# Forming the first two channel tiles together, reordering the turn to the down projection, and halving the last output tile

## The chip, the core and the metric

The kernel runs on one core of one Trainium2 chip. A core has TensorE (PE in the profile; PEld is its weight load, which overlaps), VectorE (DVE), ScalarE (ACT), GpSimd (POOL) and SyncE (SP), which here only issues transfers. Each engine takes its instructions in order and waits for others through semaphores. Operands lie in SBUF (128 partitions); matmul results lie in PSUM, in banks of 128 x 512 float32. The metric is the device time of one execution in microseconds; shorter is better.

## The reference

One transformer-like block on x (1024 tokens by 1024), in float32:

```python
h = rms_norm(x, norm1_g[l])
z = h @ w_in[l]
glu_in, q, k, v, gate_logits = jnp.split(z, SPLITS, axis=-1)
a_val, a_gate = jnp.split(glu_in, 2, axis=-1)
a = a_val * jax.nn.sigmoid(a_gate)
a = causal_depthwise_conv(a, conv_w[l], conv_b[l])          # 31 taps
a = jax.nn.silu(rms_norm(a, conv_norm_g[l]))
y_a = a @ w_conv_out[l]
...
y_b = o @ w_attn_out[l]          # o: dilated attention, 16 heads, 3 groups
g_a, g_b = jnp.split(jax.nn.sigmoid(gate_logits + gate_b[l]), 2, axis=-1)
x = x + (g_a * y_a + g_b * y_b) @ w_out[l]

h = rms_norm(x, norm2_g[l])
u = causal_depthwise_conv(h @ w_up[l], ffn_conv_w[l], ffn_conv_b[l])   # 3 taps
u_val, u_gate = jnp.split(u, 2, axis=-1)
x = x + (jax.nn.silu(u_gate) * u_val) @ w_down[l]
```

## The kernel before, in words

**Precision.** Each float32 operand of a product is split into a rounded high part and the rest (`split`, lines 77 to 80: ACT rounds, DVE subtracts). A product is three matmuls: high by high, high by low, low by high. So nearly every weight or activation costs one ACT and one DVE instruction before PE can use it. A "step" below is one such matmul, 128x128 by 128x512.

**Order.** A planner in the build lays out the order of each engine's instructions by a simulated timeline. In three stretches the order of ACT, DVE and PE is the written one (`tc.manual_schedule`): the start (line 432), attention (line 770) and the change to the feed-forward part (line 1038). `tc.issue_after(i)` ties what it encloses, on i's engine only, behind i in the order of issue; it adds no wait for i to finish.

**Start (lines 287 to 502).** The gated linear unit has eight channel tiles c of 128 channels, each with a gate part g and a value part v. For c = 0 and 1, and the first half of the tokens, PE multiplies raw x (scaled by the norm's gain) and the norm's factor is applied at the end. x arrives in eight blocks k (`xT`, 256 KB each). `w_first` holds the weights of tile 0 in four pieces, each for two k; piece 0 is loaded in two halves of columns, g and v. `raw_high`/`raw_low` (lines 363 and 366) split x's block k, `weights(k)` splits the weights of k and k+1 in four blocks of 256 columns (`whigh` line 381, `wlow` line 384; the profile shows their instructions at L382 and L386). `pair` (line 390) issues the steps of tile c, at L395. Tile 0 goes k by k as the blocks arrive, six steps each; then tile 1, whose weights come in two whole loads (`stage`, L84), goes at once, 48 steps, with the norm's spread over the rows (`spread`, L347) after 36 of them. Then follow both tiles on the second half of the tokens, and tiles 2 to 7 with the loop at line 510. Rounded weights live in the tags `whi` and `wlo`, four buffers each; tiles 0 and 1 take all four, and the next tile's rounding takes a buffer when its last reader is done. While tiles 2 and up run, DVE scales and splits the first half of x (`normed` L371, `low` L375).

**Convolution and cover.** `conv_branch` (line 538) runs on DVE beside the q, k, v products. At its end PE sums squares (`pss`, line 656). `cover(n)` (line 644) takes n steps of three matmuls from a stock of side work (the gates' products, `side_steps`); `COVER` (line 39) gives the counts: before the convolution's end, after the sum, after the spread. The rest of the stock is spent inside attention. There, pieces of gate weights wait in a queue for their split; `piece_high` (line 167) rounds one, at two places of each slot; the first is taken if more than three wait (line 789).

**Up projection and turn.** Each up tile f (22 of them) is formed by a Strassen-like scheme of products (`product`, L979 to L981). `up_rest` (line 1157) ends one: its PSUM bank X is drained at L1168, multiplied into again (third product), read at L1172, multiplied into once more (fourth product, `t4`) and drained at L1177; Y is a second bank. `up_end` (line 1143) applies the three taps (L1148, L1150) and stores the tile. The down projection (from line 1221) multiplies in six groups of two f-tiles (the last of one). Its first sweep adds into X[0..3], which lie in two double banks `dx_0` and `dx_1`; `dx_1` is the memory of the last up tile's X and Z. For groups 0 and 1, loaded early, the steps for n = 0, 1 come before those for n = 2, 3 (lines 1272 to 1275): 24 steps are free of the last up tile and 24 wait for L1177. `gsplit` and `wsplit` round the groups' operands; those of group 4 are tied behind L1177 (line 1269).

**End (lines 1349 to 1358).** The steps of the last two groups are kept back: for n = 0 to 3 nine steps on Y[n], then for n = 0 to 3 the residual is loaded, nine steps on X[n] follow (`mac`, L1247), DVE adds (L1251) and SP stores the 128x512 tile (`emit`, L1279).

Of the kernel before, what the change touches and what calls it, by code (L numbers as in the profile page):

```python
# [21 lines left out]
P = 128  # L22
# [16 lines left out]
COVER = (14, 8, 20)  # L39
# [14 lines left out]
def block_kernel(ctx: ExitStack, tc: tile.TileContext, x, xT, x0, g2, pack, mask,  # L54
# [225 lines left out]
    with tc.tile_pool(name="ph1", bufs=1) as p1:  # L280
# [11 lines left out]
        raw0 = [wp.tile([P, 1024], F32, tag="raw", bufs=4, name=f"raw_gv{n}") for n in range(2)]  # L292
        block0 = lambda k, i: raw0[k // 4][:, (k // 2 % 2) * 512 + i * 256 : (k // 2 % 2) * 512 + i * 256 + 256]

        def first_weights(k):
            if k == 0:
                for i in range(2):
                    sp.dma_start(block0(0, i), w_first[0, :, i * 256 : i * 256 + 256])
            else:
                sp.dma_start(raw0[k // 4][:, (k // 2 % 2) * 512 : (k // 2 % 2) * 512 + 512], w_first[k // 2])  # L300
# [16 lines left out]
        raw1 = []  # L317
# [56 lines left out]
        def low(half, k):  # L374
# [3 lines left out]
        wfirst = [[[wp.tile([P, 1024], F32R, tag=t, bufs=4, name=f"{t}_{n}{c}") for t in ("whi", "wlo")] for n in "gv"]  # L378
                  for c in range(2)]

        def whigh(c, which, raw, cols=slice(0, 1024)):
            act.activation(wfirst[c][which][0][:, cols], raw, AF.Copy)  # L382

        def wlow(c, which, raw, cols=slice(0, 1024)):
            hi, lo = wfirst[c][which]
            dve.tensor_tensor(out=lo[:, cols], in0=raw, in1=hi[:, cols].bitcast(F32), op=ALU.subtract)  # L386
# [3 lines left out]
        def pair(c, half, ks, passes, which):  # L390
            w = [t.rearrange("p (a b) -> p a b", a=KT) for t in wfirst[c][which]]
            o = glu0[c, half][which]
            for k in ks:
                for wa, ha in passes:
                    pe.matmul(o, w[wa][:, k, :], hT[ha][half][:, k, :],  # L395
# [36 lines left out]
        with tc.manual_schedule(engines={ENG.Activation, ENG.DVE, ENG.PE}):  # L432
# [5 lines left out]
            def weights(k):  # L438
                c = slice(k * P, k * P + 2 * P)
                for i in range(2):  # L440
                    whigh(0, i, block0(k, i), c)
                    wlow(0, i, block0(k, i), c)
# [24 lines left out]
            pair(1, 0, b, HH + HL + LH, 1)  # L467
# [213 lines left out]
    with tc.tile_pool(name="ph2", bufs=1, reuse_waits="tile") as p2:  # L681
# [88 lines left out]
        with tc.manual_schedule(engines={ENG.Activation, ENG.DVE, ENG.PE}):  # L770
            pend = []
            for at in range(len(slots) + BACK + 1):
# [16 lines left out]
                if len(pieces) > 3:  # L789
                    piece_high(2)  # L790
# [351 lines left out]
    if True:  # L1142
# [14 lines left out]
        def up_rest(f, xz, sw, gw, s4):  # L1157
# [10 lines left out]
            act.activation(uv[:, t1], X, AF.Copy)  # L1168
# [7 lines left out]
            product(X, gh[:, 4:8], gl[:, 4:8], *blk["t4"], False)  # L1176
# [241 lines left out]
```

## Time and profile before

| what | us |
|---|---|
| median of 3 runs | 1747.04 (1746.75 to 1747.27) |
| profiled execution, its own time | 1747.08 |
| its span in the profile | 1745.3 |
| PE busy / PEld busy | 1738.5 / 1449.6 |
| DVE busy / ACT busy / POOL busy | 1298.5 / 796.6 / 176.3 |

The times in the lines are microseconds from the span's start; a row of the order of time has start, duration, engine, line, operation, tiles, shapes and, in brackets, how long the engine was idle before it and what released it. A matmul's duration is longer than its share of PE, since matmuls are pipelined: the share is the distance from one start to the next. The clock that PE was granted is full throughout (9 in each of 40 slices).

### The profile page before, as it was taken

What the parts mean: (1) busy time and instruction counts of PE and PEld (TensorE: products, weight loads), DVE (VectorE), ACT (ScalarE), POOL (GpSimd) and SP (SyncE); (2) the same over time, 40 slices, a digit from 0 to 9 for tenths busy, and PEclk for the clock granted to TensorE, in tenths of its full rate; (3) what the DMA queues carried; (4) which work ended last, traced back from release to release, by engine and by line L of the source; (5) the groups of instructions that cost most, each with busy time, mean ns of one, the idle gap of its engine ahead of it and who ended that gap; (6) DMA issues with size and microseconds to landing.
All of it is one profiled execution on the core that took longest, in us unless ns stands there. A gap on an engine that the chain in (4) does not pass through costs nothing.

```text
span 1745.3 us, 22811 instructions
## 1 busy us (share of the span) xinstructions
PE 1738.5 (100%) x8214; PEld 1449.6 (83%) x8214; DVE 1298.5 (74%) x1997; ACT 796.6 (46%) x1277; POOL 176.3 (10%) x188
## 2 busy tenths in 40 slices
PE   9999999999999999999999999999999999999999
PEld 7888888888888888888888888888888888878887
DVE  5999999999766666667654564787777776879863
ACT  6411233223276666667563342555445444543431
POOL 0000231132012222222200000000000000000000
PEclk9999999999999999999999999999999999999999
DMA  7111145345686556657356576632221222498851
GB/s 300 67 49 49 49 145 169 103 142 174 175 275 180 148 161 164 181 163 229 111 186 211 167 260 254 219 119 75 95 85 72 85 84 85 138 335 324 294 175 49
DMA packets 149202, 277.00 MB, mean 159 GB/s; under 512 B 12000, under 2 KB 61536, under 8 KB 149088
## 3 DMA queue, kind: packets, MB, share of 16 engines
q1 hardware_dynamic: 146784, 269.25, 47.5%
q10 hardware_dynamic: 2304, 6.29, 0.9%
q8 instruction: 65, 1.06, 0.3%
q14 instruction: 49, 0.40, 0.1%
HBM read 202.09 MB, written 73.40 MB: 158 GB/s over the span
## 4 chain that ended last, share of the span: by engine, by line
PE 98%; DMA 1%; DVE 0%; issue 0%; ACT 0%; SPq 0%; ACTq 0%
PE dx L1247 7%; PE xz L979 6%; PE xz L980 6%; PE xz L981 6%; PE dy L1247 5%; PE qkv L128 5%; PE qkv L130 5%; PE qkv L129 5%; PE pp L721 4%; PE gate L111 3%; PE gate L113 3%; PE gate L112 3%; PE y L980 2%; PE y L979 2%; PE y L981 2%; PE o L736 2%
## 5 line engine op out<-in xcount | busy, mean ns | idle before, releaser
L80 DVE TENSOR_TENSOR pl<-pp,ph 128x512 fp32r<-128x512 f32 (+2 forms) x191 | 100.3, 552 | 91.0 <-ACT ph L79 90.8
L128 PE MATMUL qkv<-hi_qkv,hT 128*128 128x512 f32 x384 | 150.9, 395 | 0.0
L130 PE MATMUL qkv<-hi_qkv,hT 128*128 128x512 f32 x384 | 150.2, 391 | 0.0
L129 PE MATMUL qkv<-lo_qkv,hT 128*128 128x512 f32 x384 | 149.9, 391 | 0.0
L79 ACT ACTIVATE ph<-pp 128x512 fp32r<-128x512 f32 (+2 forms) x191 | 86.7, 488 | 117.4 <-PE pp L721 116.1
L706 DVE CUSTOM_DVE_ANT_0 p<-s,m 128x128 f32<-128x128 f32 (+3 forms) x120 | 90.5, 754 | 43.6 <-PE s L702 39.9
L715 POOL TENSOR_SCALAR p<-p,st 128x128 f32<-128x128 f32 (+3 forms) x120 | 91.3, 761 | 279.9 <-DVE st L714 232.2
L1150 DVE SCALAR_TENSOR_TENSOR u<-u,pk 128x1023 f32<-128x1023 f32 x88 | 112.2, 1277 | 1.0 <-ACT u L1148 0.7
L111 PE MATMUL gate<-hT,hi_gt 128*128 128x512 f32 x256 | 102.3, 400 | 0.0
L112 PE MATMUL gate<-hT,hi_gt 128*128 128x512 f32 x256 | 100.4, 392 | 0.0
L113 PE MATMUL gate<-hT,lo_gt 128*128 128x512 f32 x256 | 100.4, 393 | 0.0
L104 POOL TENSOR_TENSOR rs<-ss,mhalf 128x8 f32<-128x8 f32 x32 | 67.8, 2121 | 297.3 <-DVE ss L103 297.3
L711 ACT ACTIVATE p<-p,st 128x128 f32<-128x128 f32 (+3 forms) x120 | 93.0, 775 | 2.1 <-DVE st L706 1.2
L560 DVE SCALAR_TENSOR_TENSOR cacc<-csum,both,cacc 128x512 f32<-128x512 f32 x120 | 89.3, 745 | 0.8 <-ACT cacc L558 0.4
L560 DVE SCALAR_TENSOR_TENSOR cacc<-apad,pk,cacc 128x512 f32<-128x512 f32 x120 | 87.4, 745 | 0.0
L130 PEld LDWEIGHTS qkv<-hi_qkv,hT 128*128 128x128 f32 x384 | 72.1, 188 | 15.0
L129 PEld LDWEIGHTS qkv<-lo_qkv,hT 128*128 128x128 f32 x384 | 72.2, 188 | 14.4
L560 DVE SCALAR_TENSOR_TENSOR codd<-apad,pk,codd 128x513 f32<-128x513 f32 x112 | 83.6, 747 | 0.4 <-ACT codd L553 0.4
L80 DVE TENSOR_TENSOR lo_uv<-raw_uv,hi_uv 128x1024 fp32r<-128x1024 f32 x20 | 24.5, 1225 | 79.8 <-ACT hi_uv L79 79.8
L128 PEld LDWEIGHTS qkv<-hi_qkv,hT 128*128 128x128 f32 x384 | 72.1, 188 | 14.1
L721 PE MATMUL pp<-ident,p 128*128 128x128 f32 x540 | 78.7, 272 | 0.0
L721 PEld LDWEIGHTS pp<-ident,p 128*128 128x128 f32 x540 | 65.8, 140 | 14.5 <-DVE op L747 0.2
(362 smaller groups left out, 4849.0 us busy)
## 6 DMA issues: line engine op xcount, KB each, us to landing
wr<-w_down SPq DMA_DIRECT2D x45, 512.0 KB, 5.8
gr<-dff SPq DMA_DIRECT2D x62, 256.0 KB, 5.1
raw_qkv<-w_qkv SPq DMA_DIRECT2D x24, 512.0 KB, 5.2
dff<-u SPq DMA_DIRECT2D x22, 512.0 KB, 2.6
raw_uv<-w_up SPq DMA_DIRECT2D x21, 512.0 KB, 3.2
raw_ug<-w_up SPq DMA_DIRECT2D x20, 512.0 KB, 3.2
dv<-v SPq DMA_DIRECT2D x16, 512.0 KB, 3.2
raw_gt<-w_ch SPq DMA_DIRECT2D x16, 512.0 KB, 4.2
```

The costliest lines, as they stand in the source:

```text
L111: pe.matmul(o, hi[:, k, :], ah[:, k, :], start=(k == 0), stop=False)
L112: pe.matmul(o, hi[:, k, :], al[:, k, :], start=False, stop=False)
L113: pe.matmul(o, lo[:, k, :], ah[:, k, :], start=False, stop=(k == KT - 1))
L128: pe.matmul(ps, ah, hi[:, k % 2, :], start=(k == 0), stop=False)
L129: pe.matmul(ps, ah, lo[:, k % 2, :], start=False, stop=False)
L130: pe.matmul(ps, al, hi[:, k % 2, :], start=False, stop=(k == KT - 1))
L560: dve.scalar_tensor_tensor(out=out_, in0=src[:, i : i + size], scalar=w(i), in1=out_, op0=ALU.mult, op1=ALU.add)
L721: pe.transpose(pp[:, qb * P : (qb + 1) * P], pts[qb][:, kt * P : (kt + 1) * P], ident)
L979: pe.matmul(o, wh[:, k, :], bh[:, k, :], start=(start and k == 0), stop=False, skip_group_check=not start)
L980: pe.matmul(o, wh[:, k, :], bl[:, k, :], start=False, stop=False, skip_group_check=not start)
L981: end = pe.matmul(o, wl[:, k, :], bh[:, k, :], start=False, stop=(k == 3), skip_group_check=not start)
L1247: pe.matmul(banks[n], a[:, c], b[:, d], start=(start and i == 0 and m == 0), stop=(stop and i == nf - 1 and m == 2), skip_group_check=True)
```

## The change

1. The weights of tiles 0 and 1 are laid out by k: piece k (256 KB) has four blocks of 128 columns, g and v of tile 0, g and v of tile 1. Piece 0 is loaded in two halves, one for each tile. There are eight blocks of x and nine loads of weights in turn; the two whole loads for tile 1 go. `first_split(k)` splits a piece right behind x's block k.
2. PE goes k by k for both tiles, twelve steps each, with the spread ahead of k = 7. The split of the rows' squares and factors on ACT comes ahead of this in the text, without tile 1's roundings between. Each rounded-weight buffer now holds two k of all four columns' blocks.
3. `COVER[0]` is 15 in place of 14; in attention the first `piece_high` of a slot runs if more than two pieces wait.
4. `up_rest` also returns the drain at L1168 (`copied`) and the last matmul of the fourth product (`whole`). The roundings of groups 2, 3 and 5 are tied behind the last up tile's `copied`; those of group 4 stay behind L1177. Of the 24 free steps, the six of group 1 for n = 1 are tied behind `whole`.
5. For the last output tile (n = 3 of X) the residual is loaded first and the sum so far of its right half is added to it. Then its nine steps are issued twice with 256 columns: the left half goes on in X[3], the right half starts afresh in Y[0]. Each half is added and stored by itself, the left through ACT's queue, the right through SP's.

```diff
-COVER = (14, 8, 20)
+COVER = (15, 8, 20)
...
+        sides = lambda k: (slice(0, 256), slice(256, 512)) if k == 0 else (slice(0, 512),)
+        of_piece = lambda ts, k: ts[k // 2][:, k % 2 * 512 : k % 2 * 512 + 512]
+        raw0 = [wp.tile([P, 1024], F32, tag="raw", bufs=4, name=f"raw_gv{n}") for n in range(4)]
         def first_weights(k):
+            for i, c in enumerate(sides(k)):
+                sp.dma_start(of_piece(raw0, k)[:, c],
+                             w_first[k].rearrange("p c -> (p c)").rearrange("(i p c) -> i p c", i=len(sides(k)), p=P)[i])
         for k in range(KT):
-            if k % 2 == 0 and k > 2:
-                first_weights(k)
...
-            if k < 2:
-                first_weights(2 * k)
+            first_weights(k)
...
         for tt in range(4, 8):
-            if tt < 6:
-                raw1.append(stage(w_ch[9 if tt == 4 else 1], f"gv{tt}"))
             natural(tt)
...
+        wfirst = [[wp.tile([P, 1024], F32R, tag=t, bufs=4, name=f"{t}_gv{n}") for n in range(4)] for t in ("whi", "wlo")]
+        def first_split(k):
+            raw, hi, lo = (of_piece(t, k) for t in (raw0, *wfirst))
+            for c in sides(k):
+                act.activation(hi[:, c], raw[:, c], AF.Copy)
+                dve.tensor_tensor(out=lo[:, c], in0=raw[:, c], in1=hi[:, c].bitcast(F32), op=ALU.subtract)
...
             for k in range(KT):
-                if k % 2 == 0 and k > 2:
-                    weights(k)
                 raw_high(k)
                 raw_low(k)
-                if k < 2:
-                    weights(2 * k)
-            banks(0, 0, True)
-            for k in range(KT):
-                for passes in (HH, LH, HL) if 0 < k < 4 else (HH, HL, LH):
-                    for which in range(2):
-                        pair(0, 0, [k], passes, which)
+                first_split(k)
+            for c in range(2):
+                banks(c, 0, True)
             for tt in range(4, 8):
-                if tt < 6:
-                    whigh(1, tt - 4, raw1[tt - 4])
-                    wlow(1, tt - 4, raw1[tt - 4])
                 squares(tt)
             factors(1)
-            banks(1, 0, True)
-            pair(1, 0, range(8), HH + HL + LH, 0)
-            pair(1, 0, a, HH + HL + LH, 1)
             diagonals(1)
-            rows[1] = spread(1)
-            pair(1, 0, b, HH + HL + LH, 1)
+            for k in range(KT):
+                if k == 7:
+                    rows[1] = spread(1)
+                for c in range(2):
+                    for passes in (HH, LH, HL) if 0 < k < 4 else (HH, HL, LH):
+                        for which in range(2):
+                            pair(c, 0, [k], passes, which)
...
-                if len(pieces) > 3:
+                if len(pieces) > 2:
                     piece_high(2)
...
-            act.activation(uv[:, t1], X, AF.Copy)
+            copied = act.activation(uv[:, t1], X, AF.Copy)
...
-            product(X, gh[:, 4:8], gl[:, 4:8], *blk["t4"], False)
+            whole = product(X, gh[:, 4:8], gl[:, 4:8], *blk["t4"], False)
...
-            return last_u
+            return copied, whole, last_u
...
-            with tc.issue_after(last_u.ins) if fs is groups[-2] else ExitStack():
+            with tc.issue_after((last_u if fs is groups[-2] else copied).ins) if fs in groups[2:] else ExitStack():
...
                     for i, gw in enumerate(first2):
-                        mac(X, *gw, len(fs), i == 0, False, only)
+                        if only[0] or not i:
+                            mac(X, *gw, len(fs), i == 0, False, only)
+                        else:
+                            mac(X, *gw, len(fs), False, False, only[:1])
+                            with tc.issue_after(whole.ins):
+                                mac(X, *gw, len(fs), False, False, only[1:])
...
+        left, right = slice(0, 256), slice(256, 512)
+        r3 = residual(0, 3, 1)
+        tt(r3[:, right], X[3][:, right], r3[:, right], add)
...
-        for n in range(4):
+        for n in range(3):
             r = residual(0, n, 1)
...
+        for banks, cols, queue in ((X, left, act), ([None] * 3 + [Y[0]], right, sp)):
+            for i, (p2, p4, nf, last) in enumerate(ends):
+                mac(banks, *p4, nf, i == 0 and cols is right, last, [3], cols)
+            tt(r3[:, cols], banks[3][:, cols], r3[:, cols], add)
+            emit(r3, 0, 3, 1, cols, queue)
```

`mac` and `emit` take the columns as an argument, `emit` the queue as well; `pair` reads its weights through `of_piece`.

More of the change, by code (lines that the diff above doesn't have):

```diff
@@ L1207, in block_kernel @@
                 if f:
-                    last_u = up_rest(f, *r)
+                    copied, whole, last_u = up_rest(f, *r)
                 else:
@@ L1238, in gsplit, with mac @@
             return hi, lo
-        def mac(banks, g, w, nf, start, stop, only=None):
+        def mac(banks, g, w, nf, start, stop, only=None, cols=slice(0, 512)):
             (gh, gl), (wh, wl) = g, w
@@ L1244, in mac @@
                     c = slice(i * 512 + n * P, i * 512 + n * P + P)
-                    d = slice(i * 512, i * 512 + 512)
+                    d = slice(i * 512 + cols.start, i * 512 + cols.stop)
                     for m, (a, b) in enumerate(((gh, wh), (gh, wl), (gl, wh))):
-                        pe.matmul(banks[n], a[:, c], b[:, d], start=(start and i == 0 and m == 0),
+                        pe.matmul(banks[n][:, cols], a[:, c], b[:, d], start=(start and i == 0 and m == 0),
                                   stop=(stop and i == nf - 1 and m == 2), skip_group_check=True)
@@ L1388, in _layout @@
     xT = np.ascontiguousarray(a["x"][0].reshape(2, 512, KT, P).transpose(0, 2, 3, 1))
-    first = w_ch[[8, 0]].reshape(2, P, 4, 256).transpose(2, 1, 0, 3).reshape(4, P, 512)
+    first = w_ch[[8, 0, 9, 1]].transpose(2, 1, 0, 3)
+    first = np.concatenate([first[0, :, :2].ravel(), first[0, :, 2:].ravel(), first[1:].ravel()]).reshape(KT, P, 512)
     return {
```

29 lines of the change are left out of this document (5 added, 24 removed).

## The prediction

> **What bounds the kernel now.** I read the page first, then who waits for whom on TensorE, then the order of time, engine by engine, at the three places the edits touch: the start, the turn from up to down projection, the end.
>
> ```profile
> span 1745.3 us, 22811 instructions
> ...
> PE 1738.5 (100%) x8214; PEld 1449.6 (83%) x8214; DVE 1298.5 (74%) x1997; ACT 796.6 (46%) x1277; POOL 176.3 (10%) x188
> ```
>
> ```profile
> PE glu L395 <- ACT hT L361: 1.2, 1, 1.2
> PE early L435 <- POOL ones L326: 1.0, 1, 1.0
> PE dx L1247 <- ACT u L1177: 0.7, 1, 0.7
> PE xz L979 <- DVE u L1172: 0.2, 1, 0.2
> ```
>
> TensorE (PE) has an instruction in flight all through the span, and its list of waits has these four rows and no more. The change takes no multiplication away, so it can win only what PE idles: one stall at the start, two at the turn, and the tail after the last matmul. With what these places hold below (1.88 + 1.42 + 0.6) the ceiling is about 4 us. 0.2% of the time is 3.5 us, about what a measurement of this kernel can tell from no change.
>
> **Start.** The first matmuls are paced by loads; PE, then ACT, then DVE, and one row of the chain that ended last:
>
> ```profile
> 4.56 0.50 PE L395 MATMUL glu<-hT,whi_g 128*128 128x512 f32 x1
> 5.08 0.51 PE L395 MATMUL glu<-hT,whi_v 128*128 128x512 f32 x1
> 5.42 0.39 PE L395 MATMUL glu<-hT,whi_g 128*128 128x512 f32 x1
> ...
> 6.10 0.39 PE L395 MATMUL glu<-hT,wlo_v 128*128 128x512 f32 x1
> 7.70 0.50 PE L395 MATMUL glu<-hT,whi_g 128*128 128x512 f32 x1 [1.21 <-ACT hT L361]
> ```
>
> ```profile
> 6.92 0.72 ACT L361 ACTIVATE hT<-xT,g1c 128x512 fp32r<-128x512 f32 x1 [1.90 <-DMA xT<-xT]
> 7.55 0.40 ACT L382 ACTIVATE whi_g<-raw_gv 128x256 fp32r<-128x256 f32 x1
> ```
>
> ```profile
> 5.32 0.42 DVE L386 TENSOR_TENSOR wlo_v<-raw_gv,whi_v 128x256 fp32r<-128x256 f32 x1
> 7.68 0.75 DVE L367 SCALAR_TENSOR_TENSOR hT<-xT,g1c,hT 128x512 fp32r<-128x512 f32 x1 [1.94 <-ACT hT L361]
> ```
>
> ```profile
> 46.61 5.44 PE gluv L395 x24
> ```
>
> Two rows each of ACT and DVE at the turn, needed there again and for the price of 512 columns here, and a stretch (its columns: start and end, length, busy time of PE, PEld, DVE, ACT, POOL, clock, DMA share, GB/s):
>
> ```profile
> 1523.51 1.05 ACT L79 ACTIVATE hi_a<-wr 128x1024 fp32r<-128x1024 f32 x1
> 1524.46 0.58 ACT L1168 ACTIVATE u<-xz 128x512 f32<-128x512 f32 x1
> ```
>
> ```profile
> 1530.19 2.60 DVE L1150 SCALAR_TENSOR_TENSOR u<-u,pk 128x1023 f32<-128x1023 f32 x2
> 1532.71 0.68 DVE L1172 TENSOR_TENSOR u<-xz,p 128x512 f32<-128x512 f32 x1
> ```
>
> ```profile
> 12.00:26.00 14.00, 14.00 (x66) 11.67 (x65) 5.73 (x9) 8.13 (x13) 1.03 (x1) 1.00 1.04 411
> ```
>
> In a stream a 512-column matmul takes 5.44/24 = 0.227 us of PE. After a pause the first takes 0.34 (5.08 to 5.42), 0.11 more. So PE loses 0.29 (4.56 to 5.08, less 0.227), 0.11, then 1.37 (6.10 to 7.70) and 0.11 again: 1.88 us. It then waits nowhere until the turn.
>
> With the change, step k=0 has twelve matmuls instead of six. The left weight block holds gate and value columns of tile 0, so one rounding serves the first two and the wait at 5.08 goes: twelve from 4.56 end at 4.56 + 12 x 0.227 + 0.11 = 7.39. Step k=1 needs weights of its own now, issued behind x's second block. In that place of the queue stands, in the old order, a piece of the same 256 KB (for k=2 and 3), and ACT takes it at 7.55 without idle time, so it had landed. Rounding 512 columns takes about 0.6 (0.58 at 1524.46), so PE gets k=1 at 7.55 + 0.6 + 0.07 = 8.22: lost 0.83 and 0.11. The low part of these weights follows raw_low on DVE, from about 8.36 (7.68 + 0.68), 0.68 long as the two-operand step at 1532.71, so to 9.04; with a hand-over of 0.04 PE has it at 9.08, and after two high steps asks for it at 8.79: 0.29 and 0.11 more. In all 0.11 + 0.94 + 0.40 = 1.45 lost, and the **start gains 0.43**. Bounds: 1.88, if nothing waits; a loss of 0.2, if the weights land one transfer later (256 KB at 411 GB/s is 0.64).
>
> Later loads are no limit: a step needs 512 KB, 1.28 us at 411 GB/s, against 12 x 0.227 = 2.72 us of PE. The queue carries the same bytes up to the rows of x for the norm; two more issues lie beside landings. The 84 matmuls ahead of the norm's spread stay 84, so what follows moves up unchanged; if the squares were late instead, that would cost their lateness, but the same bytes stand ahead of them.
>
> **The price of holding both tiles' weights.** All four pairs of rounded-weight buffers now serve both tiles until the last 24 matmuls (46.61 to 52.05). DVE, its stretch, the sum over 63 to 467 us in five stretches, and the end of the convolution:
>
> ```profile
> 40.46 1.23 DVE L80 TENSOR_TENSOR lo_g<-raw_g,hi_g 128x1024 fp32r<-128x1024 f32 x1 [1.12 <-ACT hi_g L79]
> ...
> 48.86 1.21 DVE L80 TENSOR_TENSOR lo_g<-raw_g,hi_g 128x1024 fp32r<-128x1024 f32 x1
> ```
>
> ```profile
> 44.50:62.80 18.30, 17.45 (x26) 1.00 0.25 87
> ```
>
> ```profile
> sum 404.00, PE 404.00 PEld 334.47 DVE 384.00 ACT 114.92 POOL 67.79; mean PE 80.80 PEld 66.89 DVE 76.80 ACT 22.98 POOL 13.56
> ```
>
> ```profile
> 466.15 0.69 DVE L571 TENSOR_TENSOR sqacc<-sqacc,codd 128x512 f32<-128x512 f32 x1 [1.06 <-ACT codd L570]
> 468.34 1.84 PE L656 MATMUL pss<-ones,sqacc 128*128 128x1 f32 x16
> ```
>
> Channel tile 2 was rounded as soon as tile 0 let go (40.46). Now its first buffer is free only after six of the last 24, 46.61 + 1.36 + 0.2 = 48.2; hi (1.05, as at 1523.51) and lo (1.23) then end at 50.5 at the earliest, and PE wants them from 52.05. All of it moves up 0.43 together, so 1.5 us are left and I charge **nothing**; its cover is the other 18 of the 24. But DVE is dense there (17.45 of 18.30 us), so two subtractions, 2.45 us, that used to fill idle time now push the convolution back. DVE is busy 384 of the 404 us up to 467, so that can reach the convolution's end, where PE fetches the sum of squares: DVE ended at 466.84, PE came 1.50 later. Now PE comes 0.43 earlier by the start and 3 x 0.227 = 0.68 later by the gate step that COVER puts in front (moved, not added: it is taken from attention, where PE has work throughout); DVE ends 2.45 - 0.43 = 2.02 later if its 20 us of idle take up none of it. Slack: 1.50 + 0.25 - 2.02 = -0.27. I take half, **0.15 lost**; bounds 0, and 0.7 if the earlier start gives DVE nothing. Rounding a piece once three wait, in place of four, moves ACT work by a slot; attention has no row among PE's waits: 0.
>
> **Turn.** L1168 (the row at 1524.46) is the drain now called copied, L1177 the last drain. PE:
>
> ```profile
> 1532.86 0.39 PE L1247 MATMUL dx<-early,early 128*128 128x512 f32 x1
> 1533.44 0.50 PE L979 MATMUL xz<-blk_t,hi_s3g 128*128 128x512 f32 x1 [0.20 <-DVE u L1172]
> ...
> 1536.07 0.39 PE L981 MATMUL xz<-blk_t,lo_s3g 128*128 128x512 f32 x1
> 1537.14 0.50 PE L1247 MATMUL dx<-early 128*128 128x512 f32 x1 [0.69 <-ACT u L1177]
> ```
>
> The second pair of output banks shares memory with the last up tile, so it waits for L1177. All 24 free steps on the first pair were used before the last product, hence two stalls: 1532.86 to 1533.44 is 0.35 over the pitch, 1536.07 to 1537.14 is 0.84, each with 0.11 for the restart: 1.41, say 1.42 with rounding. The change keeps six steps, 1.36 us, behind the last product; drain and hand-over need 0.84 + 0.227 = 1.07, so the second stall goes. The first would grow by the 1.36 taken from it, if the third product started no earlier. But behind copied, the rounding at 1523.51 no longer delays L1168, so that product can follow the one on y at once, and 18 steps (4.1 us) stand between its end and L1172's answer. The tie is issue order on ACT alone; behind it queue the high parts for groups 2 and 3, of which PE asks the first once the 24 steps on the second pair are through, 5.4 us after 1537.14. I take the whole **1.42**; bounds: that, and a loss of 0.40 (second stall's 0.95 gone, first longer by 1.36). Late next is the low part for group 2, on DVE behind two L1150 (2.60); these follow L1177 and move up with it.
>
> **End.** PE in attention, the tail, and the landing of the last stores:
>
> ```profile
> 535.33 0.28 PE L702 MATMUL s<-kl,q 128*128 128x256 f32 x1
> 535.44 0.40 PE L111 MATMUL gate<-hT,hi_gt 128*128 128x512 f32 x1
> ```
>
> ```profile
> 1741.21 0.39 PE L1247 MATMUL dx<-hi_a,gl_t 128*128 128x512 f32 x1
> 1741.64 0.69 DVE L1251 TENSOR_TENSOR res<-dx,res 128x512 f32<-128x512 f32 x1 [1.35 <-PE dx L1247]
> ```
>
> ```profile
> DMA to landing us min/median/max: 2.0/2.1/3.5
> ```
>
> Nine matmuls become 18 of 256 columns at 0.11 to 0.115 (535.33 to 535.44; half of 0.227 is 0.113): 2.07 for 2.04, +0.03. The last addition shrinks from 0.69 to about 0.42 (128x256 at 5.32): -0.27. The last store halves: a gain between 0 (nothing but latency) and 0.32 (128 KB at 411 GB/s); I take the middle, 0.16. **End: 0.40 gained**, bounds 0.2 and 0.6. The added first addition (0.42) and the earlier load lie beside the 36 matmuls on y; uncovered they cost 0.42 and the landing of 2.0.
>
> The Trainium skill (TensorE: Matmul & The Clock Gate, Back-to-back issue gap) speaks against halves: with a weight load for each matmul it gives about 81 ns for 128 columns and 131 for 512, so on a straight line (an estimate) 256 columns cost 0.75 of 512. By that 18 would take 3.06 us, and the end would lose 0.6. The trace's 0.11 beside 0.227 decides otherwise.
>
> **Sum**, against the profiled execution's own 1747.08 (span 1745.3 and 1.78 around it; 0.04 above the median shown): -0.43 + 0.15 - 1.42 - 0.40 = -2.10, so **1745.0**.
>
> **Rivals.** (1) The turn's order hardly changes: L1168 comes no earlier and the first stall takes what the second gives. For it: the order there is the planner's. Against: the rounding that stood ahead is tied behind. +0.40 in place of -1.42: 1746.8. (2) Tile 2's low part is queued on DVE behind the normalisation of the first half. It decides once that part ends after about 52; behind all of the dense stretch to 62.8, plus 1.23, it ends at 64.0 and PE stands some 11.7 us: 1756.7; with 2.1 us to lose, the kernel is slower than before from an end at 54.3 on. Against: at 48.86 such a subtraction was let in between. (3) The start gives its full 1.88 and the sum of squares waits for nothing: 1743.4. (4) The left half, sent by ACT's queue, lands late: its addition ends about 1.0 before the right one's, so with the 3.5 that the slowest of these stores took against 2.0 it lands 0.5 after the right half; the end then gives nothing: 1745.4.
>
> **Chances.** Forecast 0.56, (1) 0.18, (2) 0.10, (3) 0.08, (4) 0.08. The range runs from just above (3), 1743.5, through (4), (1) and the smaller waits of kind (2) to 1747.8. Faster by more than 0.2% (under 1743.5) 0.07, nearly all of (3); slower by more (over 1750.5) 0.08, most of (2); within 0.85.
>
> **What would show it.** PE with twelve matmuls from 4.56, a pause from about 7.4 to 8.2 and a short one near 9; no pause at channel tile 2; the sum of squares straight behind a gate step; the third product directly behind y's and no wait of PE on L1172 or L1177; a last addition of 0.42 and the end some 0.4 sooner after the last matmul. I am wrong if PE's list of waits has a new row longer than 1 us, or if the turn's two rows stay.

## The result, and the profile after

The changed kernel takes 1744.39 us (median of 21 runs, 1743.99 to 1745.69) against 1746.93 (median of 21 runs made beside them, 1745.97 to 1748.45): ratio 0.9986, 95% interval 0.998 to 0.9992. That is 2.54 us or 0.14% less: within the 0.2% that I counted as no change, though the interval leaves 1 out. Forecast were 2.10 less and 1745.0. The two profiled executions differ by 2.58 (1747.08 and 1744.50).

The head of the page of the changed kernel, and its list of who waits for whom on PE, whole:

```profile
span 1742.7 us, 22830 instructions
...
PE 1738.4 (100%) x8223; PEld 1451.5 (83%) x8223; DVE 1299.6 (75%) x1998; ACT 797.4 (46%) x1276; POOL 174.4 (10%) x188
```

```profile
PE early L427 <- POOL ones L320: 1.0, 1, 1.0
```

Three of the four rows are gone and none has come. PE is as busy as before; it idles less. Where, is read from the order of time on PE, at four instructions that both kernels have. (Line numbers are 5 to 21 lower in the changed kernel: L395 is now L387, L979 to L981 are L958 to L960, L1172 is L1151, L1177 is L1156, L1247 is L1226.) Before, then after:

```profile
25.55 0.61 PE L347 MATMUL psr<-dg,ones 128*128 128x128 f32 x4
...
1524.69 0.39 PE L981 MATMUL y<-blk_b,lo_s 128*128 128x512 f32 x1
...
1542.71 0.39 PE L1247 MATMUL dx<-hi_a,gh_b 128*128 128x512 f32 x1
```

```profile
25.07 0.38 PE L341 MATMUL psr<-dg,ones 128*128 128x128 f32 x2
...
1523.97 0.39 PE L960 MATMUL y<-blk_b,lo_s 128*128 128x512 f32 x1
...
1540.52 0.39 PE L1226 MATMUL dx<-hi_a,gh_b 128*128 128x512 f32 x1
...
1739.14 0.28 PE L1226 MATMUL dx<-hi_a,gl_t 128*128 128x256 f32 x1
```

The first is the norm's spread (84 steps stand ahead of it in both), the second the last step on y of the last up tile, the third the first step of the down projection's group 2, the fourth the last matmul (1741.21 before). They cut the span into five stretches:

| stretch on PE | before | after | difference | forecast |
|---|---|---|---|---|
| start, to the spread | 25.55 | 25.07 | -0.48 | -0.43 |
| spread to the last y | 1499.14 | 1498.90 | -0.24 | +0.15 |
| turn: last y to group 2 | 18.02 | 16.55 | -1.47 | -1.42 |
| group 2 to the last matmul | 198.50 | 198.62 | +0.12 | +0.03 |
| last matmul to the span's end | 4.08 | 3.57 | -0.51 | -0.43 |
| sum | 1745.29 | 1742.71 | -2.58 | -2.10 |

This table says where time went, which a median can't: the median of the kernel before alone lay between 1746.42 and 1746.93 in its five sets of runs here. But each column is one execution. In kernels with the same parts the third and fourth stretches mostly repeat within a few hundredths (e5 below is an exception); the first two don't.

**Start.** PE, ACT and the stretch from 4.6 to 7.2 (columns as in the stretches of the prediction):

```profile
0.98 4.21 PE L427 MATMUL early<-ones 128*128 128x128 f32 x18 [0.98 <-POOL ones L320]
4.84 2.05 PE L387 MATMUL glu<-hT,whi_gv 128*128 128x512 f32 x4
6.69 0.82 PE L387 MATMUL glu<-hT,wlo_gv 128*128 128x512 f32 x2
7.35 1.09 PE L387 MATMUL glu<-hT,whi_gv 128*128 128x512 f32 x4
8.28 0.62 PE L387 MATMUL glu<-hT,wlo_gv 128*128 128x512 f32 x2
8.74 0.62 PE L387 MATMUL glu<-hT,whi_gv 128*128 128x512 f32 x2
```

```profile
6.04 0.72 ACT L355 ACTIVATE hT<-xT,g1c 128x512 fp32r<-128x512 f32 x1 [0.76 <-DMA xT<-xT]
6.71 0.63 ACT L377 ACTIVATE whi_gv<-raw_gv 128x512 fp32r<-128x512 f32 x1
```

```profile
4.60:7.20 2.60, 2.60 (x9) 2.12 (x9) 1.55 (x4) 1.58 (x3) 0.00 (x0) 1.00 1.01 324
```

The gain has the size of the forecast, but not its course. Four steps from 4.84 last 2.05 us, four from 7.35 only 1.09: until about 7.1 a step costs 0.43, not 0.227. The column of the granted clock says 1.00 all the same. And x's second block was there at 6.04, not 6.92, so k = 1 waited for nothing. Experiments below separate the two.

**Holding both tiles' weights.** ACT, DVE and PE at channel tile 2, then the sum of squares:

```profile
47.85 1.05 ACT L79 ACTIVATE hi_g<-raw_g 128x1024 fp32r<-128x1024 f32 x1
```

```profile
50.32 1.21 DVE L80 TENSOR_TENSOR lo_g<-raw_g,hi_g 128x1024 fp32r<-128x1024 f32 x1
...
467.62 0.68 DVE L550 TENSOR_TENSOR sqacc<-sqacc,codd 128x512 f32<-128x512 f32 x1
```

```profile
52.31 0.39 PE L113 MATMUL glug<-hT,lo_g 128*128 128x512 f32 x1
...
468.49 1.88 PE L635 MATMUL pss<-ones,sqacc 128*128 128x1 f32 x16
```

The low part of tile 2 is ready at about 51.5 and asked for at 52.31. DVE ends the convolution 1.46 later than before (468.30 and 466.84), PE comes 0.15 later, and 0.19 are left.

**Turn.** ACT and DVE, then PE at the third product, the fourth, and behind it:

```profile
1521.77 0.58 ACT L1147 ACTIVATE u<-xz 128x512 f32<-128x512 f32 x1
1522.25 1.99 ACT L79 ACTIVATE hi_a<-wr 128x1024 fp32r<-128x1024 f32 x2
...
1538.71 1.06 ACT L79 ACTIVATE gh_b<-gr 128x1024 fp32r<-128x1024 f32 x1 [1.59 <-DMA gr<-dff]
```

```profile
1528.84 1.28 DVE L1129 SCALAR_TENSOR_TENSOR u<-u,pk 128x1023 f32<-128x1023 f32 x1 [0.19 <-ACT u L1127]
1530.04 0.68 DVE L1151 TENSOR_TENSOR u<-xz,p 128x512 f32<-128x512 f32 x1
1530.64 1.27 DVE L1129 SCALAR_TENSOR_TENSOR u<-u,pk 128x1022 f32<-128x1022 f32 x1
```

```profile
1526.47 0.39 PE L958 MATMUL xz<-blk_t,hi_s3g 128*128 128x512 f32 x1
...
1531.00 0.39 PE L958 MATMUL xz<-blk_t,hi_s3g 128*128 128x512 f32 x1
...
1533.72 0.39 PE L1226 MATMUL dx<-early,early 128*128 128x512 f32 x1
```

The roundings now stand behind the drain (1522.25 behind 1521.77), L1151 stands between the two L1129 in place of behind both and comes 2.67 earlier (1.95 counted from the last y), and PE passes from product to product without a pause. It does not put the third product straight behind y, as I had it: ten free steps lie between 1523.97 and 1526.47, eight between the products, six behind.

**End.** PE, DVE and the last store:

```profile
1735.05 0.28 PE L1226 MATMUL dy<-hi_a,gh_t 128*128 128x256 f32 x1
...
1736.12 0.40 PE L1226 MATMUL dx<-hi_a,gh_t 128*128 128x512 f32 x1
...
1738.19 0.28 PE L1226 MATMUL dx<-hi_a,gh_t 128*128 128x256 f32 x1
```

```profile
1739.46 0.42 DVE L1230 TENSOR_TENSOR res<-dx,res 128x256 f32<-128x256 f32 x1 [0.38 <-PE dx L1226]
```

```profile
1739.91 0.38 ACTq L1264 DMA_DIRECT2D out<-res  x1
```

The planner put the right half first, then the n = 2 tile, then the left half. Nine matmuls of 256 columns take 1.07 (1735.05 to 1736.12). From the last matmul to the span's end are 3.57: the last addition is 0.27 shorter, it begins 0.32 after the last matmul's start and not 0.43, and from the issue of the store to the end pass 2.80 (2.94 before).

Up to the last matmul's start the two halves take 2.02 (1.07 and 0.95), the whole tile before took 1.81: 0.21 more. The table has only 0.12, because the kernel before lost 0.09 just behind group 2's first step, where the group's low part came late (two steps on PE lie 0.32 apart, from 1543.62). That small wait belongs to the turn, and it is gone. So the end brings 0.30 net, and the turn 1.56.

### The profile page after: what moved, and what is told of

It reads as the page before. It is cut to its first block, busy times and chain, and to the rows that moved or that the text cites. A ratio compares the mean times of both kernels' runs of the same rounds, so it can differ in the third digit from the quotient of the medians.

```text
span 1742.7 us, 22830 instructions
## 1 busy us (share of the span) xinstructions
PE 1738.4 (100%) x8223; PEld 1451.5 (83%) x8223; DVE 1299.6 (75%) x1998; ACT 797.4 (46%) x1276; POOL 174.4 (10%) x188
## 3 DMA queue, kind: packets, MB, share of 16 engines
q10 hardware_dynamic: 2448, 6.42, 0.9%
## 4 chain that ended last, share of the span: by engine, by line
PE 100%; DVE 0%; issue 0%; POOL 0%; POOLq 0%
PE dx L1226 7%; PE xz L959 6%; PE xz L958 6%; PE xz L960 6%; PE dy L1226 5%; PE qkv L130 5%; PE qkv L128 5%; PE qkv L129 5%; PE pp L700 4%; PE gate L111 3%; PE gate L113 3%; PE gate L112 3%; PE y L959 2%; PE y L960 2%; PE y L958 2%; PE o L715 2%
## 5 line engine op out<-in xcount | busy, mean ns | idle before, releaser
L1129 DVE SCALAR_TENSOR_TENSOR u<-u,pk 128x1023 f32<-128x1023 f32 x88 | 112.1, 1276 | 1.2 <-ACT u L1127 0.9
L539 DVE SCALAR_TENSOR_TENSOR cacc<-csum,both,cacc 128x512 f32<-128x512 f32 x120 | 89.2, 744 | 1.2 <-ACT cacc L537 0.9
L539 DVE SCALAR_TENSOR_TENSOR cacc<-apad,pk,cacc 128x512 f32<-128x512 f32 x120 | 87.4, 742 | 0.0
L539 DVE SCALAR_TENSOR_TENSOR codd<-apad,pk,codd 128x513 f32<-128x513 f32 x112 | 83.4, 746 | 0.0
```

The costliest lines, as they stand in the source:

```text
L539: dve.scalar_tensor_tensor(out=out_, in0=src[:, i : i + size], scalar=w(i), in1=out_, op0=ALU.mult, op1=ALU.add)
```

## The experiments

Columns: median of eleven runs (ten for e11), its difference to the kernel before on the same chip and the interval of the ratio; then, from the one profiled execution, the spread's start, the turn and the tail as in the table above.

| run | median | difference | interval of the ratio | spread | turn | tail |
|---|---|---|---|---|---|---|
| e1_ties | 1746.04 | -0.44 | 0.9987 to 1.0005 | 24.93 | 17.53 | 3.57 |
| e2_kept | 1745.56 | -0.92 | 0.9985 to 1.0003 | 25.04 | 17.63 | 3.58 |
| e3_nocover | 1745.29 | -1.19 | 0.9986 to 1.0003 | 25.09 | 16.55 | 3.57 |
| e4_turn | 1745.54 | -0.94 | 0.9985 to 1.0003 | 25.23 | 16.89 | 4.08 |
| e5_start | 1747.53 | +1.11 | 0.9996 to 1.0013 | 26.01 | 17.53 | 3.95 |
| e6_end | 1745.90 | -0.52 | 0.9987 to 1.0005 | 25.14 | 18.01 | 3.55 |
| e7_quarters | 1746.09 | -0.33 | 0.9987 to 1.0005 | 24.62 | 16.55 | 3.36 |
| e8_endsp | 1744.38 | -2.04 | 0.998 to 0.9998 | 25.92 | 16.55 | 3.54 |
| e9_nostart | 1744.95 | -1.48 | 0.9984 to 1.0002 | 25.18 | 16.55 | 3.55 |
| e10_actload | 1744.20 | -2.23 | 0.9978 to 0.9995 | 24.49 | 16.55 | 3.55 |
| e11_nowarm | 1745.58 | -0.85 | 0.9985 to 1.0003 | 25.88 | 16.55 | 3.57 |
| e12_halfload | 1744.25 | -2.32 | 0.9976 to 0.9994 | 24.43 | 16.55 | 3.54 |

By their medians only e8, e10 and e12 are told from the kernel before; the other intervals include 1. What the parts do is therefore read from the traces, one execution of each kernel.

### The turn: ties alone, kept steps alone, the turn alone

e1, the changed kernel without the six kept steps:

```diff
-                        if only[0] or not i:
-                            mac(X, *gw, len(fs), i == 0, False, only)
-                        else:
-                            mac(X, *gw, len(fs), False, False, only[:1])
-                            with tc.issue_after(whole.ins):
-                                mac(X, *gw, len(fs), False, False, only[1:])
+                        mac(X, *gw, len(fs), i == 0, False, only)
```

> The changed kernel with its ties behind the drain at L1147, but without the six steps kept for the end. Theory: the ties close the first stall, the six steps the second. So PE does not wait at the third product; all 24 free steps are used up before the last product, and the second pair of banks waits for the drain L1156: a pause of about 0.95 (drain 0.58, hand-over, restart, as in the kernel before). Time: 1744.4 + 0.95 = 1745.4. Rival (the first rival of the prediction, that ties change nothing): both rows of the kernel before return, at L958/L959 and at L1226, 1.4 in all: 1745.8. Second rival: no pause, 1744.4.

e2, the changed kernel without the ties:

```diff
-            with tc.issue_after((last_u if fs is groups[-2] else copied).ins) if fs in groups[2:] else ExitStack():
+            with tc.issue_after(last_u.ins) if fs is groups[-2] else ExitStack():
```

> The changed kernel with the six steps kept for the end, but without the ties: two roundings of 1.05 stand ahead of L1147 on ACT, two subtractions of 1.23 go onto DVE before L1151. Theory: PE then waits once, at the fourth product (the one that needs L1151), by about 1.0 and 0.11 for the restart, and not behind it: 1744.4 + 1.1 = 1745.5. First rival of the prediction: the first stall takes all that the second gave, 0.35 + 1.36 + 0.11 = 1.8 at one place: 1746.2. Second rival: the planner's order absorbs it, no pause, 1744.4.

PE's waits at the turn, e1, then e2:

```profile
PE dx L1226 <- ACT u L1156: 0.7, 1, 0.7
```

```profile
PE xz L958 <- DVE u L1151: 0.7, 1, 0.7
```

One row each at the turn, and each the one that was named. The turn takes 17.53 with the ties alone and 17.63 with the kept steps alone, against 16.55 with both and 18.02 with neither: 0.98 and 1.08 above the changed kernel, where 0.95 and 1.1 were expected. Together they bring 1.47, singly 0.49 and 0.39: each alone mostly moves the stall to the other place.

The 0.49 of the ties is not secured by this. The turn of before has its first stall in two traces (18.02; 18.01 in e6), but in e5, which also has neither edit, that stall is absent and the turn takes 17.53. There PE comes to the last y at 1525.35, 0.66 later than before, while DVE ends L1151 at 1533.04, in time for the step on PE at 1533.74. So what the turn's part is worth depends on how PE stands to DVE in the execution: 1.47 against before, 0.98 against e5. The second stall is there in every trace without the kept steps.

e4 has the kernel before with the turn's edits (both diffs above, in the other direction, and the drain and the last product handed on by `up_rest`) and nothing else.

> The kernel before with the turn's part of the change alone. Theory: both rows (PE dx <- ACT u, PE xz <- DVE u) go and nothing comes in their place, 1.42 by the prediction and up to 1.6 by the trace of the changed kernel, whose 25 us there hold 1.59 less of PE's idle time: 1747.0 - 1.5 = 1745.5. Rival: part of the gain in that window came from the other parts of the change (another order of transfers), then one row of 0.2 to 0.7 stays: 1746.3.

Both rows went, but the turn takes 16.89, 0.34 more than in the changed kernel. ACT, then PE in e4:

```profile
1539.65 1.06 ACT L79 ACTIVATE gh_b<-gr 128x1024 fp32r<-128x1024 f32 x1 [2.58 <-DMA gr<-dff]
```

```profile
1540.77 0.50 PE L1247 MATMUL dx<-hi_a,gh_b 128*128 128x512 f32 x1
...
1542.03 0.50 PE L1247 MATMUL dx<-hi_a,gl_b 128*128 128x512 f32 x1
```

ACT had been idle for 2.58 until group 2's operands had come back from memory. PE waits for their high part (0.28 ahead of 1540.77) and again for their low part (0.23 ahead of 1542.03), which DVE makes from the high part. The second wait lies behind the turn as I cut it: from the last y to the last matmul e4 takes 215.80, the kernel before 216.52: a gain of 0.72 and not 1.13. In the changed kernel the operands came at 1538.71. There the high part is ready 0.75 before PE asks for it (1539.77 and 1540.52), the low part 0.39 (1541.04 and 1541.43). So the low part on DVE is the next to be late, as I had named it, but in e4 it is late through this load and not through DVE's queue. The rival, a small remaining wait, holds for this execution. In e8 the low part alone is late and costs 0.14 behind a turn of 16.55.

### The fifteenth step ahead of the sum of squares, and the start alone

e3, the changed kernel with two numbers set back:

```diff
-COVER = (15, 8, 20)
+COVER = (14, 8, 20)
...
-                if len(pieces) > 2:
+                if len(pieces) > 3:
```

> The changed kernel with 14 steps ahead of the sum of squares as before, and the first rounding of a slot taken from more than three. Theory: in the changed kernel's trace DVE ends the convolution at 468.30 and PE comes to the sum of squares at 468.49; without the fifteenth step PE comes 0.68 sooner, at 467.81, so a row pss <- DVE sqacc of 0.5 and a restart of 0.11 appear: 1744.4 + 0.6 = 1745.0. By the prediction's own terms (slack -0.27 with the step) the wait would be 0.95. Rival: DVE makes up the time earlier, no row, 1744.4; then the fifteenth step was not needed.

e5 is the kernel before with the loads, roundings and order of the start (items 1 and 2 of the change), and 14 steps.

> The kernel before with the start's part alone (both tiles together, loads by k; 14 steps ahead of the sum of squares). Theory of the prediction: PE loses 1.45 at the start in place of 1.88, since it waits for the weights of k = 1, whenever PE's pitch is halved; the wait at the sum of squares is 0.5 to 0.95. Rival, from the changed kernel's trace: no step waits for loads; the loss is that the first twelve steps run at 0.43 until some time between 4 and 7.2 us. Where the pitch falls to 0.227 late (after 6.5), the first step of k = 1 starts at about 8.7 as there, a loss of 1.46; where it falls at 4.0 as in the trace of the kernel before, the first step of k = 1 starts at 7.4 and the loss is 0.2 to 0.7, so the start gains 1.2 to 1.7. In the sum: 1747.0 - 0.45 + 0.6 = 1747.1 with a late fall, 1746.1 with an early one.

PE's waits in e3, then in e5:

```profile
PE pss L635 <- DVE sqacc L550: 0.5, 1, 0.5
PE glu L387 <- ACT whi_gv L377: 0.3, 1, 0.3
```

```profile
PE glu L387 <- ACT whi_gv L377: 0.8, 1, 0.8
PE dx L1226 <- ACT u L1156: 0.7, 1, 0.7
PE pss L635 <- DVE sqacc L550: 0.5, 1, 0.5
```

The step is needed: without it PE waits 0.5 and restarts, in both (0.5 as the changed kernel's trace says, not the 0.95 of the prediction's terms). The rows on L387 are waits for the weights of k = 1. The start alone is not faster in its median (+1.11, interval across 1): it pays this wait, and its profiled execution had x's second block late.

That block is the key to the start. e3 had it at the same time as the kernel before (6.93, and 6.92 there). ACT, then PE in e3:

```profile
6.93 0.72 ACT L355 ACTIVATE hT<-xT,g1c 128x512 fp32r<-128x512 f32 x1 [1.16 <-DMA xT<-xT]
```

```profile
8.23 0.73 PE L387 MATMUL glu<-hT,whi_gv 128*128 128x512 f32 x2 [0.30 <-ACT whi_gv L377]
...
9.10 0.73 PE L387 MATMUL glu<-hT,wlo_gv 128*128 128x512 f32 x2
...
25.09 0.72 PE L341 MATMUL psr<-dg,ones 128*128 128x128 f32 x5
```

This is the course of the prediction: k = 1 at 8.23 (forecast 8.22), then a short wait for the low part, and the spread at 25.09 in place of 25.55, 0.46 earlier. The time from ACT taking the block to the spread, in every trace with the first weights on SP's queue, like x:

| start | block taken by ACT | spread | between |
|---|---|---|---|
| old: before, e4, e6, e9 | 6.92, 6.59, 6.51, 6.43 | 25.55, 25.23, 25.14, 25.18 | 18.63, 18.64, 18.63, 18.75 |
| new, block sets it: e1, e3, e5, e7, e8, e11 | 6.76, 6.93, 7.85, 6.45, 7.75, 7.73 | 24.93, 25.09, 26.01, 24.62, 25.92, 25.88 | 18.17, 18.16, 18.16, 18.17, 18.17, 18.15 |
| new, PE's pitch sets it: after, e2 | 6.04, 6.42 | 25.07, 25.04 | 19.03, 18.62 |

The new start is worth 0.46 for an equal landing, where the landing sets the time. The landing moves by 1.8 us between executions (6.04 to 7.85), and the mean spread of the first seven new starts, 25.24, is no better than that of the four old ones, 25.28. In after and e2 the block came early, but the pitch stayed at 0.43 until about 7.1, which holds the spread at about 25.05 however early the block is. The old start is held by such a pitch too: in e6, slow until 7.1, PE goes from k = 0 to k = 1 without a pause at 7.36, and the spread is at 25.14. There the new start is worth 0.1. So its gain lies between 0.1 and 0.46 by landing and pitch, and that it makes the kernel faster over many executions is not shown.

### The start taken back, and the early products

e9 is the changed kernel with the start and the 14 steps of before.

> The changed kernel with the start of before (tile 0 first, 14 steps ahead of the sum of squares), turn and end as changed. Theory of the prediction: the new start is worth 0.43 less 0.15, so this kernel takes 1744.4 + 0.3 = 1744.7. Rival, from PE's idle time in the first 25 us of the ten traces so far (old start 3.56, 3.24, 3.15, mean 3.31; new start 3.08, 2.94, 3.05, 3.11, 4.02, 2.63, 3.93, mean 3.25): the new start is worth nothing that holds from one execution to the next, 1744.4, and PE's idle time there is 3.1 to 3.6. Neither start has a wait at the sum of squares here.

The spread stands at 25.18 with the block at 6.43; the new start would have had it at 24.60 or, with a pitch late to fall, 25.05. The median is 0.56 above the changed kernel's, but the two were measured apart and their intervals overlap: it agrees with 0.46 and doesn't exclude 0.

e11 shows the pitch by itself:

```diff
-WARM = 9
+WARM = 0
```

> The changed kernel without its nine early products on ones (they leave nothing in the output). Theory: PE's pitch of 0.43 for 512 columns lasts until PE has been busy for some 3 to 6 us (in the traces so far from the first product at 0.98 to between 4.0 and 7.2), whatever the loads do. Without the early products that count begins at the first step at about 4.6: the pitch falls between 7.6 and 11, 7 to 15 steps run at 0.43 in place of 0 to 5, and of the 0.2 that each loses 0.2 to 1.0 in all is hidden by waits for loads: 0.4 to 2.0 slower, 1744.8 to 1746.4. Rival: the slow first steps are paced by weights and loads and not by a clock; then the early products don't matter and the time stays within 0.2 of 1744.4. The Trainium skill (TensorE: Matmul & The Clock Gate, What's actually happening) says the first: half the clock until a window of about 3.4 us has been busy, the window running freely.

PE in e11:

```profile
4.53 2.08 PE L387 MATMUL glu<-hT,whi_gv 128*128 128x512 f32 x4 [4.53 <-ACT whi_gv L377]
6.40 1.05 PE L387 MATMUL glu<-hT,wlo_gv 128*128 128x512 f32 x2
7.26 1.56 PE L387 MATMUL glu<-hT,whi_gv 128*128 128x512 f32 x4
```

Eight steps at 0.43, to 8.4, 3.9 us after PE's first work. All that these steps read was there by 5.8 (DVE's last subtraction for k = 0 runs from 5.36 to 5.78), so the rival falls: they don't wait for weights or loads. In no trace with early products is the pitch slow beyond 7.2, so its fall goes with when PE began to work, as far as one trace shows it.

What the early products are worth is not shown. The median gains 0.85, against 2.04 in e8 and 2.54 in the changed kernel, but its interval includes 1 and the three were measured apart. And the trace shows no loss: x's second block came late, at 7.73, and the spread stands 18.15 behind it, as in e8 (18.17). The twelve steps of k = 0 end at 9.11 (8.74 in after), and only an early block would let that count, for some 0.4 (an estimate from these two numbers).

### The end

e6 is the kernel before with item 5 of the change alone.

> The kernel before with the end's part alone. Theory: -0.40 by the prediction (last addition 0.69 to 0.42, half a store), -0.53 by the changed kernel's trace: from the last matmul's start to the span's end 3.56 in place of 4.09: 1746.5. The planner puts the right half ahead of the n = 2 tile and the left half last. Rival: nothing is gained, since the tail is the store's latency, 4.0 from the last matmul: 1746.9.

The tail is 3.55, against 4.08 with a whole tile (before and e4; 3.95 in e5), and the stretch ahead of it costs 0.23 more (198.73; 198.50 before). The turn is unchanged at 18.01. Net 0.30.

e7, in quarters:

```diff
-        for banks, cols, queue in ((X, left, act), ([None] * 3 + [Y[0]], right, sp)):
+        quarters = [slice(i * 128, i * 128 + 128) for i in range(4)]
+        for banks, cols, queue in zip((X, [None] * 3 + [Y[0]], [None] * 3 + [Y[1]], [None] * 3 + [Y[2]]), quarters, (act, sp, act, sp)):
```

> The changed kernel with the last tile in four pieces of 128 columns in place of two of 256: 36 matmuls of 128 columns in place of 18 of 256. Theory: a matmul of this kind has a floor of 0.11 of PE (the early 128-column ones run at 0.11, the 256-column ones at 0.115 to 0.12), so 36 cost 3.96 in place of 2.07, +1.9; the last addition shrinks from 0.42 to about 0.29, -0.13: 1744.4 + 1.8 = 1746.2. Rival: the cost goes with the columns, 36 x 0.057 = 2.04, and the last quarter only shortens the tail: 1744.2. By the Trainium skill (TensorE: Matmul & The Clock Gate, Back-to-back issue gap), 81 ns for each, it would be 36 x 0.081 = 2.92, +0.85: 1745.1.

PE in e7, the nine matmuls of one quarter and the first of the next:

```profile
1738.55 0.27 PE L1226 MATMUL dx<-hi_a,gh_t 128*128 128x128 f32 x1
...
1739.56 0.27 PE L1226 MATMUL dy<-hi_a,gh_t 128*128 128x128 f32 x1
```

1.01 for nine, 0.112 each: in a row of matmuls, each with its own weights, 128 columns cost as much as the 0.11 to 0.12 that 256 columns take, not half. A single one of 128 columns behind one of 512 takes 0.06 (1738.16 to 1738.22), so it is the row that has the floor. The stretch grew to 200.47, by 1.85; the tail fell by 0.2; the median is 1.71 above that of e8 on the same chip.

e8 sends the left half through SP's queue (`left, sp` in place of `left, act`).

> The changed kernel with the left half stored through SP's queue, like the right one, in place of ACT's. Theory: the issue takes 0.33 on SP and 0.38 on ACT, the landing is the same 2.0, so the end moves by less than 0.1: 1744.4. Rival (the fourth of the prediction): a store by ACT's queue lands later; then the end comes 0.3 to 1 sooner with SP: 1743.4 to 1744.1.

Tail 3.54 against 3.57: the queue matters by no more than the difference of issue (0.33 and 0.38). The fourth rival falls.

### Loads of the start on two queues

e10 and e12 ask whether x's second block can be had sooner. e10:

```diff
-                sp.dma_start(of_piece(raw0, k)[:, c],
+                (sp if k else act).dma_start(of_piece(raw0, k)[:, c],
```

> The changed kernel with the two halves of weight piece 0 loaded through ACT's queue, ahead of its table load, in place of SP's, so that SP issues x's second block at about 1.1 in place of 2.1. Theory: what PE waits for at k = 1 is x's second block, which ACT got between 6.04 and 7.85 in the traces so far, with PE idle 0.2 to 1.0 behind the first twelve steps wherever the pitch had fallen to 0.227 before 6; one microsecond earlier on the queue, it is there before 6 and this wait goes. PE's idle time in the first 25 us: 2.5 to 3.0 in place of 2.6 to 4.0; time 1744.4 - 0.4 = 1744.0. Rival: bytes and not issues set the landings, so x's first block and piece 0 now share the engines and both come later; the first matmul starts after 4.84, and nothing is gained: 1744.4 to 1744.8.

e12 has `(act if i else sp)` in that place, only the second half on ACT's queue, and e8's store.

> The changed kernel with only the second half of weight piece 0 loaded through ACT's queue, and the left half of the last tile stored through SP's. Theory: x's second block is issued at about 1.6 (2.1 in the changed kernel, 1.17 with both halves on ACT's queue), and x's first block shares the engines with 128 KB less than with both halves there, so the first step starts between 4.84 and 5.23, and the norm's spread reaches PE at 24.5 or sooner (24.49 with both halves, 25.24 mean of the seven traces of the changed start): time 1744.2 or 0.2 below. At the end up to 0.07 by the shorter issue. Rival: the order of landing and not the issue decides; x's second block lands as late as in the changed kernel (ACT takes it after 6.0), the spread stays at 25 and the time at 1744.4.

ACT, then PE in e12:

```profile
5.29 0.71 ACT L355 ACTIVATE hT<-xT,g1c 128x512 fp32r<-128x512 f32 x1
```

```profile
5.13 1.29 PE L387 MATMUL glu<-hT,whi_gv 128*128 128x512 f32 x4 [0.51 <-ACT whi_gv L377]
```

Theory and rival both had a part: the first step starts later (5.23 in e10, 5.13 in e12; 4.84 in after), since x's first block comes later, but the second is there at 5.3 to 5.6, earlier than in any other trace, and the spread comes at 24.49 and 24.43, 0.6 before the changed kernel's. In part this may be luck: in both traces the pitch fell at 3.9, as early as in any, and twelve steps that are slow until 7.1 hold the spread at 25.07 in after, where they start earlier (4.84). That two queues alone bring the 0.6 is not shown. The medians, 1744.20 and 1744.25, are below both kernels'; against the changed kernel the difference is within the scatter, against before it is -2.23 and -2.32.

## Why the prediction was right

- **Start, 0.43 gained.** Right in mechanism and size for a landing as in the kernel before: e3 repeats its steps (8.22 and 8.23) and gives 0.46. That the changed kernel's own profile shows 0.48 is luck: it has another cause, a block 0.88 earlier and steps at 0.43. What the working left out is the slow pitch: "twelve from 4.56 end at 7.39" took PE's rate from a trace in which it had risen by 4.1; here the twelve ended at 8.74.
- **Weights held, 0; sum of squares, 0.15 lost.** The first holds, with 0.8 to spare, and the second rival falls. The second was mis-sized: DVE ended 1.46 later, not 2.02. It begins the convolution 1.68 later (the first L539 at 64.89; L560 at 63.21 before), and its idle time takes up 0.2 of that on the way. So the slack stayed positive (0.19, not -0.27). That the step must be there is shown by e3 and e5.
- **Turn, 1.42 gained.** 1.47 measured, but 0.98 if e5's turn is taken as the one before: how long the first stall is differs between executions. That ties and kept steps are both needed is shown by e1 and e2; the first rival falls. The detail that the third product follows y at once, with 18 steps behind it, was wrong and did not matter (ten steps lie ahead of it, eight behind): L1151 came early because the planner put it between the two taps of L1129. What is late next was named rightly, but not why (e4: a load).
- **End, 0.40 gained.** 0.30 measured, 0.51 in the tail less 0.21 ahead of it; e6 has 0.30 too. The matmuls cost more than the 0.03 of the working: 18 at 0.119 are 2.14 for 2.04, so 0.10. The rest of the 0.21 and of the tail's gain is one thing, that the last matmul is itself shorter (by 0.11). The addition gave the 0.27 forecast, the half store 0.14 for 0.16. The order of the halves was the planner's, not the text's.
- **The rest.** The stretch between spread and turn was 0.24 shorter. In all traces it lies between 1498.65 and 1499.34, and kernels with the same parts differ there by as much (e4 1498.65, e6 1499.22, both with the start of before). I take 0.24 for scatter; its causes were not followed up.

The sum was 0.44 short of the measured 2.54, and of the 0.5 between the profiled executions 0.39 is this stretch. Turn and end, which the experiments carry, make up some 1.9 of the 2.58; the rest is the start and this stretch, where other executions differ by as much.

## What to carry to other kernels

Where medians scatter by more than an edit can bring, compare the lengths of stretches between instructions that all variants have: the changed turn repeated to 0.01 us in eight traces, while the median of one kernel moved by 0.5. One trace is not enough for it, though: the old turn took 18.0 in two and 17.53 in a third. Two stalls in series share one supply of work: cured singly, each hands most of its time to the other (0.49 and 0.39 gained, 1.47 together). And a step that waits for a transfer at the start is to be judged at equal landing, since the landing itself moves by more than the edit.

## What the runs showed of the hardware

In all fourteen traces PE starts slowly: 0.21 for 128 columns, and 0.43 for 512 where such steps come early enough. With first work at 0.98 this lasts until 3.88 at the earliest (e10) and about 7.1 at the latest (after), with first work at 4.53 until 8.4 (e11); after that 0.11 and 0.227. The Trainium skill (TensorE: Matmul & The Clock Gate, What's actually happening) describes this: half the clock until a window of some 3.4 us, which runs freely, has been busy. The traces fit half the pace and a time that varies, 2.9 to 6.2 us after the first work, the shortest less than such a window; the granted clock in the profile doesn't show it, it reads 1.00 meanwhile (4.6 to 7.2 in after). In a row of matmuls, each with its own weight load, one took 0.112 at 128 columns (e7), 0.119 at 256 and 0.227 at 512 (after).
